# Sums of the last projection's weights computed early and kept in DRAM; eight of eleven pairs by seven products

## The chip, the cores and the metric

The kernel runs on one core of one Trainium2 chip. The metric is the device time of one execution in microseconds (us), as the median of several executions; lower is better.

## The reference, cut to what matters

One decoder layer over 512 tokens of width 1024. Three token mixers (gMLP "a", sparse attention "b", the recurrent block "c") are gated and merged, then comes a SwiGLU feed-forward part. What the change touches is the last matrix product of all, and in time the third branch.

```python
y = w_o( sum_k sigmoid(gate_k(h)) * (branch_k @ W_br_k) );  x = x + rms_norm(y)
...
f = (jax.nn.silu(f_gate) * f_up) @ w_ffn_out      # 512 x 2816  times  2816 x 1024
x = x + rms_norm(f)
...
def compress(t, pe, w1, w2):                      # of keys and of values, in branch b
    return jax.nn.gelu(flat @ w1) @ w2
```

## The kernel before, in words

**Split products.** Every large product is done in three passes on TensorE: each operand is written as a high part (rounded to fp32r) and a low part (the rest), and hi·hi, hi·lo and lo·hi are summed in PSUM. `split` (L112 to L122) makes the parts: ScalarE (ACT) copies the high part (L117), VectorE (DVE) subtracts it for the low one (L122). Weights come in 512 KB tiles of 128x1024, loaded on SyncE's queue (SP, L182) into `raw` (two buffers), then split into `hi` and `lo` (three buffers each). A main matmul is 128x128 by 128x512.

**The order of the work** is fixed when the program is built. Each engine, and each queue of DMA issues, runs its own list strictly in that order, and waits on semaphores for the others. Generators are interleaved by `run(main, side)` (L1612): `main` is a list of generators that issue matmuls, and at every yield `side` is stepped.

**The third branch.** `run(ahead, seq(compress(1), gmlp_prep(), v_norm()))` runs the eight `branch_part("c", j)` and the gate parts between them (14 parts in `ahead`), one 512 KB weight tile each; `run([u_tile(j) ...])` follows with eight more. Beside them `compress(1)` (L650) makes compressed keys or values of branch b: matmuls into a bank `tr` (L670), a GELU of which DVE does two steps into `chid` (L678, L680) and ACT the steps between (L677, L679), copies into `h4` (L694, eight) and small matmuls on `h4` (L698). The one before it, `compress(0)`, ends in the matmuls of L685, which read its `chid`. `merged` (L1035) is DVE's step that reads each branch tile out of PSUM. The hidden layer's weights `w` come by two loads of 1 MB on ACT's queue (L652).

**The last projection.** The 2816 rows of `w_ffn_out` are 11 pairs of 256 rows; tile `w_fo[i]` holds pair i for output columns 0 to 511, `w_fo[11+i]` for the others. The first NP = 5 pairs are multiplied directly (`block`, L1388): `down_first` (L1390) does columns 0 to 511, `down_last` (L1570) the rest. Of these `down_last` takes the last LAST = 4 tiles together, block of tokens by block of tokens, and closes each block (`close`, from L1579: the square on ACT into `junk`, the norm on DVE, the stores) while the next is multiplied. The other NS = 6 pairs go through seven products of half size instead of eight, on sums of quarters of the activations and of the weights (class `Seven`, products at L1493). `prep_a` (L1428) loads both tiles of a pair, makes the two weight sums on DVE (L1435, L1436), stores one of them in a DRAM tile `t2` (L1437), and splits four quarters; these feed the first sweep (four products a pair). `prep_b` (L1458) loads the other two quarters and `t2` (L1463 to L1465, 256 KB each), subtracts `t2` from both (L1470, L1471) and splits three quarters for the second sweep (three products a pair). A sweep works on one pair while the one after the next is prepared. Sums of the activations are made at L1447, L1448, L1478 and L1479.

Of the kernel before, what the change touches and what calls it, by code (L numbers as in the profile page):

```python
# [50 lines left out]
def hybrid_block(ctx: ExitStack, tc: tile.TileContext, A, out):  # L51
# [41 lines left out]
    def slab(name, dt=F32, tag="slab", shape=(4, S)):  # L93
        pool, bufs = (merge if tag == "m" else big, TAGS[tag]) if tag in TAGS else phase_pool[tag]
        return pool.tile([128, *shape], dt, tag=tag, name=nm(name), bufs=bufs)
# [20 lines left out]
    def split(src, hi, lo, lo_eng=None):  # L116
        res["hi"] = SC.activation(hi, src, AF.Copy)  # L117
        e = lo_eng or V
        if e is GP:
            GP.tensor_sub(lo, src, f32(hi))  # L120
        else:
            res["lo"] = V.tensor_sub(lo, src, f32(hi))  # L122
# [36 lines left out]
            wlist += [(A["w_vp"][1, i], None) for i in range(2)]  # L159
    w_branch(1)  # L160
    wlist += [(A["w_o"][k], t) for k, t in enumerate(["h"] * 4 + ["f"] + ["m"] * 2 + [None])]
    HEAD, LAST, LASTV = 2, 4, 2
    WAIT, STEP = (5, 6, 7), (1, 1, 2)
    wlist += [(A["w_fi"][i], None if i < 2 else "h") for i in range(2 * HEAD)]
    wstop = [len(wlist)]
    NS = 6
    NP = NFF // 2 - NS
    wlist += [(A["w_fo"][i], "y" if i < 2 else None) for i in range(NP)]
    wfirst_half = len(wlist)
# [383 lines left out]
    def v_norm():  # L553
        st = const0([128, 4, 2, 6], "bnst")
        ag = const.tile([128, 4, 2], F32, name="bnag")
        sd = const.tile([128, 2, 4], F32, name="bnsd")
        for c in range(4):
            with tc.issue_after(res["lo"].ins):
                for i in range(2):
                    V.bn_stats(st[:, c, i, :], gm["v"][c // 2][:, c % 2, i * 512:(i + 1) * 512])  # L560
            V.bn_aggr(ag[:, c, :], st[:, c])
            yield

        V.tensor_mul(sd[:, 1], ag[:, :, 1], rmul[:, 2])
        rsqrt(sd[:, 0], sd[:, 1], 4, 1.0, 4 * EPS)
        V.tensor_mul(sd[:, 0], sd[:, 0], rstd)
        V.scalar_tensor_tensor(sd[:, 1], ag[:, :, 0], -1.0, sd[:, 0], op0=OP.mult, op1=OP.mult)
        for c in range(4):
            v = gm["v"][c // 2][:, c % 2, :]
            V.tensor_scalar(v, v, sd[:, 0, c:c + 1], sd[:, 1, c:c + 1], op0=OP.mult, op1=OP.add)  # L570
            yield

    ya = {}
# [834 lines left out]
    class Seven:  # L1408


        def __init__(self):
            self.keep = slab("kS", tag="h", shape=(NS, 256))
            self.t2 = tc.dram_tile([NS, 128, 512], F32, name="t2")
            self.w, self.x = {}, {}
            self.turn = 0

# [11 lines left out]
        def prep_a(self, s):  # L1428

            i = NP + s  # L1430
            r0, r1 = self.raw()
            SY.dma_start(r0, A["w_fo"][i])
            SY.dma_start(r1, A["w_fo"][NFF // 2 + i])
            yield
            V.tensor_sub(r1[:, :512], r1[:, 512:], r1[:, :512])  # L1435
            V.tensor_add(r1[:, 512:], r0[:, :512], r1[:, :512])  # L1436
            SY.dma_start(self.t2[s], r1[:, 512:])  # L1437
            yield
            w1 = self.stream()
            split(r0, *w1)  # L1440
            yield
            w2 = slab("w2", F32R, "mo", (2, 1024))
            w2 = w2[:, 0], w2[:, 1]
            split(r1, *w2)
            yield
            F, k = fpair(i), self.keep[:, s]
            V.tensor_sub(F[:, 256:512], F[:, :256], F[:, 256:512])  # L1447
            V.tensor_sub(k, F[:, 768:], F[:, 256:512])  # L1448
            yield
            u = slab("ua", F32R, "mo", (2, 1024))  # L1450
            split(F[:, :768], u[:, 0, :768], u[:, 1, :768])
            split(k, u[:, 0, 768:], u[:, 1, 768:])
            for p, x, w, o in (("P1", 0, w1, 0), ("P7", 256, w2, 0), ("P2", 512, w1, 512), ("P6", 768, w2, 512)):
                self.x[s, p] = [u[:, l, x:x + 256] for l in range(2)]
                self.w[s, p] = [t[:, o:o + 512] for t in w]
            yield

        def prep_b(self, s):  # L1458

            i = NP + s  # L1460
            r, t2 = self.raw()
            t2 = t2[:, :512]
            SY.dma_start(r[:, :512], A["w_fo"][i, :, 512:])  # L1463
            SY.dma_start(r[:, 512:], A["w_fo"][NFF // 2 + i, :, 512:])
            SY.dma_start(t2, self.t2[s])  # L1465
            yield
            w1 = [t[:, :512] for t in self.stream()]
            split(r[:, 512:], *w1)
            yield
            V.tensor_sub(r[:, 512:], r[:, 512:], t2)  # L1470
            V.tensor_sub(r[:, :512], r[:, :512], t2)  # L1471
            yield
            w2 = slab("w3", F32R, "mo", (2, 1024))
            w2 = w2[:, 0], w2[:, 1]
            split(r, *w2)
            yield
            F, k = fpair(i), self.keep[:, s]
            V.tensor_add(F[:, 256:512], k, F[:, :256])  # L1478
            V.tensor_sub(F[:, 512:768], F[:, 512:768], k)  # L1479
            yield  # L1480
            u = slab("ub", F32R, "mo", (2, 1024))
            split(F[:, 256:], u[:, 0, :768], u[:, 1, :768])
            for p, x, w, o in (("P5", 0, w2, 512), ("P3", 256, w1, 0), ("P4", 512, w2, 0)):
                self.x[s, p] = [u[:, l, x:x + 256] for l in range(2)]
                self.w[s, p] = [t[:, o:o + 512] for t in w]
            yield
# [19 lines left out]
    def sweeps(sv):  # L1506

        b = res["b0"]
        zu = slab("zu", tag="fx")
        z, u3 = [zu[:, n, :] for n in range(2)], [zu[:, n + 2, :] for n in range(2)]  # L1510
        for n in range(2):
            SC.activation(z[n], b[2 + n], AF.Copy)
        X2, X1, X3 = b[:2], [bank("mm") for _ in range(2)], [bank("tr") for _ in range(2)]
        X4 = [bank("mm") for _ in range(2)]
        steps = iter(())

        def go(n=9):
            for _ in range(n):
                next(steps, None)

        for s in range(NS):
            end = s >= NS - 2
            for p, X in (("P1", X1), ("P6", X3), ("P7", X4)) + (() if end else (("P2", X2),)):
                sv.product(s, p, X, s == 0 and p != "P2")
                go(2)
            go()
            if not end:
                steps = sv.prep_a(s + 2)
        for s in (NS - 2, NS - 1):
            sv.product(s, "P2", X2, False)  # L1530
            steps = sv.prep_b(s - NS + 2)
            if s == NS - 2:
                p1, u2 = [[row("p1") for _ in range(2)] for _ in range(2)]
                for n in range(2):
                    SC.activation(p1[n], X1[n], AF.Copy)
                for n in range(2):
                    V.tensor_add(X3[n], X3[n], p1[n])
                for n in range(2):
                    SC.activation(u2[n], X3[n], AF.Copy)
                for n in range(2):  # L1540
                    V.tensor_add(X4[n], X4[n], u2[n])
                for n in range(2):
                    SC.activation(u3[n], X4[n], AF.Copy)
            go()
        for n in range(2):
            close_first(n, X2[n], p1[n])
        X5 = [bank("mm") for _ in range(2)]
        for s in range(NS):
            for p, X in (("P5", X5), ("P3", X3), ("P4", X4)):
                sv.product(s, p, X, s == 0 and p == "P5")  # L1550
                go(2)
                if s == NS - 1 and p == "P5":
                    p5 = [row("p5") for _ in range(2)]
                    for n in range(2):
                        SC.activation(p5[n], X5[n], AF.Copy)
                    for n in range(2):
                        V.tensor_add(X5[n], X5[n], u3[n])
                if s == NS - 1 and p == "P3":
                    for n in range(2):
                        V.tensor_add(X3[n], X3[n], p5[n])  # L1560
            go()
            if s + 2 < NS:
                steps = sv.prep_b(s + 2)
            elif s + 2 == NS:
                wstop[0] = len(wlist)
        for n in range(2):
            close_first(2 + n, X4[n], z[n])
        res["b1"] = X3 + X5
# [70 lines left out]
    def seq(*gens):  # L1639
        for g in gens:  # L1640
            for _ in g:
                yield 1
# [26 lines left out]
    run([gate_part("c", 0), compress(0), gate_part("c", 1)], side)  # L1669
    yc["h"], yc["l"] = ([yc[n, k // 4][:, k % 4, :] for k in range(NK)] for n in "hl")  # L1670
    ahead = [x for j in range(8) for x in [branch_part("c", j, yc)] + ([gate_part("c", j + 2)] if j < 6 else [])]
    run(ahead, seq(compress(1), gmlp_prep(), v_norm()))
    run([u_tile(j) for j in range(8)])
    next_phase(1)
    next_banks(1)
    for tag in ("sc", "sc", "o"):
# [120 lines left out]
```

## Time and profile before

| what | before |
|---|---|
| median of 3 runs (lowest, highest) | 1118.88 us (1118.82, 1119.29) |
| the profiled execution: its time | 1118.62 us |
| the profiled execution: its span | 1116.9 us |
| TensorE (PE) busy | 1106.0 us, 99% |
| VectorE (DVE) busy | 825.0 us, 74% |
| ScalarE (ACT) busy | 612.7 us, 55% |
| DMA, mean over the span | 110 GB/s |

The profiled execution's time is its span and 1.7 us around it. In rows of the timeline the columns are: start in us, duration in us, engine, line, operation, output and inputs, shapes, how often (xN: merged), and in brackets the idle time before it and what ended it. Rows of the stretches give busy time and count for each engine, then the granted clock, the DMA share and the rate. Matmuls overlap in the pipe: one is 0.39 us long, and the next starts before it ends. "Qs" after an engine's name (SPq, ACTq) are its DMA issues.

### The profile page before, as it was taken

To read this page: it belongs to the slowest core of one execution; us is meant where nothing else is said; L and a number is where in the kernel's file an instruction comes from. 1 tells how busy PE (TensorE), PEld (TensorE's weight loads), DVE (VectorE), ACT (ScalarE), POOL (GpSimd) and SP (SyncE) were. 2 spreads that over 40 slices of the span, in tenths; PEclk is the share of its full clock that TensorE was granted. 3 is DMA by queue.
4 is the path that set the end of the run, shared out by engine and by line. 5 is a ranking of instruction groups with operands and counts; after the bars stand their busy time and mean duration, and the time that the engine had idled before them with its cause. 6 is when DMAs were issued, how large, how long until landed. Compare 5 with 4: busy or idle time off the path is not lost.

```text
span 1116.9 us, 16130 instructions
## 1 busy us (share of the span) xinstructions
PE 1106.0 (99%) x6164; PEld 958.8 (86%) x6164; DVE 825.0 (74%) x1514; ACT 612.7 (55%) x1107; POOL 22.4 (2%) x39
## 2 busy tenths in 40 slices
PE   9999999999999999999999999999999999999997
PEld 8888788888889888888788788888999999998876
DVE  5987858263574888978888844468998888877894
ACT  6757574232344696957967633345655555563651
POOL 1000202100000000000000000000000000000000
PEclk9999999999999999999999999999999999999999
DMA  8332316323223312222221253353233323356351
GB/s 320 103 94 76 113 57 236 103 76 94 94 76 105 94 49 61 63 58 77 66 57 57 65 200 94 106 177 113 76 114 114 114 79 130 114 174 211 96 198 75
DMA packets 36572, 122.36 MB, mean 110 GB/s; under 512 B 4304, under 2 KB 4592, under 8 KB 35344
## 3 DMA queue, kind: packets, MB, share of 16 engines
q1 hardware_dynamic: 34048, 111.61, 31.0%
q10 hardware_dynamic: 2160, 9.04, 2.3%
q8 instruction: 48, 0.79, 0.3%
q0 software_dynamic: 288, 0.69, 0.2%
q14 instruction: 28, 0.23, 0.1%
HBM read 112.42 MB, written 5.77 MB: 106 GB/s over the span
## 4 chain that ended last, share of the span: by engine, by line
PE 91%; DVE 4%; ACT 3%; issue 1%; DMA 1%; DVEq 0%; ACTq 0%
PE mm L221 40%; PE mm L1292 18%; PE mm L526 4%; PE mm L1388 4%; PE sc L857 3%; PE o L895 3%; PE mm L1077 3%; PE tr L882 3%; PE mm L1493 2%; PE mm L763 2%; PE mm L234 2%; PE tr L670 1%; PE tr L1388 1%; PE tr L449 1%; PE tr L1493 1%; DVE lo L122 1%
## 5 line engine op out<-in xcount | busy, mean ns | idle before, releaser
L117 ACT ACTIVATE hi<-raw 128x1024 fp32r<-128x1024 f32 (+1 forms) x132 | 136.1, 1032 | 180.8 <-PE mm L221 99.8
L122 DVE TENSOR_TENSOR lo<-raw,hi 128x1024 fp32r<-128x1024 f32 (+1 forms) x132 | 157.1, 1192 | 90.1 <-ACT hi L117 83.7
L221 PE MATMUL mm<-hh,hi 128*128 128x512 f32 x504 | 199.6, 396 | 0.0
L221 PE MATMUL mm<-hh,lo 128*128 128x512 f32 x504 | 197.2, 391 | 0.0
L221 PE MATMUL mm<-hl,hi 128*128 128x512 f32 x504 | 196.9, 391 | 0.0
L221 PEld LDWEIGHTS mm<-hh,lo 128*128 128x128 f32 x504 | 94.7, 188 | 19.8
L221 PEld LDWEIGHTS mm<-hl,hi 128*128 128x128 f32 x504 | 94.7, 188 | 18.6 <-issue 0.2
L221 PEld LDWEIGHTS mm<-hh,hi 128*128 128x128 f32 x504 | 94.7, 188 | 18.2 <-issue 0.2
L863 ACT ACTIVATE P<-P,ast 128x128 f32<-128x128 f32 (+3 forms) x128 | 70.6, 553 | 16.0 <-DVE ast L861 15.4
L1292 PE MATMUL mm<-S,g 128*128 128x256 f32 x600 | 76.9, 283 | 0.0
L1292 PEld LDWEIGHTS mm<-S,g 128*128 128x128 f32 x600 | 74.2, 192 | 0.1
L861 DVE CUSTOM_DVE_ANT_0 P<-sc,mask 128x128 f32<-128x128 f32 (+3 forms) x128 | 58.1, 482 | 8.3 <-PE sc L857 8.1
L122 DVE TENSOR_TENSOR pl<-tr,ph 128x512 fp32r<-128x512 f32 x80 | 53.5, 685 | 12.5 <-ACT ph L117 10.6
L117 ACT ACTIVATE ph<-tr 128x512 fp32r<-128x512 f32 x80 | 46.0, 590 | 11.9 <-PE tr L882 9.2
L857 PE MATMUL sc<-K,q 128*128 128x512 f32 (+2 forms) x192 | 49.6, 365 | 0.1
L1292 PE MATMUL mm<-A,g 128*128 128x256 f32 x360 | 46.6, 283 | 0.0
L882 PE MATMUL tr<-ident,P 128*128 128x128 f32 x320 | 45.2, 273 | 0.3 <-ACT P L873 0.3
L882 PEld LDWEIGHTS tr<-ident,P 128*128 128x128 f32 x320 | 38.0, 140 | 8.2 <-ACT P L873 0.8
L1292 PEld LDWEIGHTS mm<-A,g 128*128 128x128 f32 x360 | 44.8, 192 | 0.1
L1292 PE MATMUL mm<-S,hi 128*128 128x256 f32 x240 | 44.6, 283 | 0.0
L1292 PE MATMUL mm<-A,hi 128*128 128x256 f32 x240 | 44.2, 283 | 0.0
L857 PEld LDWEIGHTS sc<-K,q 128*128 128x128 f32 x192 | 33.3, 188 | 6.4 <-DVE ast L861 1.2
(397 smaller groups left out, 2439.1 us busy)
## 6 DMA issues: line engine op xcount, KB each, us to landing
raw<-in_w_in SPq DMA_DIRECT2D x64, 512.0 KB, 3.6
raw<-in_w_fi SPq DMA_DIRECT2D x44, 512.0 KB, 3.6
raw<-in_w_br SPq DMA_DIRECT2D x24, 512.0 KB, 3.5
raw<-in_w_fo SPq DMA_DIRECT2D x22, 512.0 KB, 3.7
w<-in_cw ACTq DMA_DIRECT2D x4, 1024.0 KB, 6.0
raw<-in_w_o SPq DMA_DIRECT2D x8, 512.0 KB, 3.6
raw<-in_w_v SPq DMA_DIRECT2D x7, 512.0 KB, 5.0
raw<-in_w_fo SPq DMA_DIRECT2D x12, 256.0 KB, 3.2
```

Of the source, the lines that this page charges most:

```text
L117: res["hi"] = SC.activation(hi, src, AF.Copy)
L122: res["lo"] = V.tensor_sub(lo, src, f32(hi))
L221: res["mm"] = PE.matmul(ps[:m, n0:n1], w[:, k * 128:k * 128 + m], x[k][:, n0:n1], start=(t == 0), stop=(t == 3 * NK - 1))
L526: res["mm"] = PE.matmul(b[c], x[k][:, c * 128:(c + 1) * 128], w[:, kk * 512:kk * 512 + 512], start=(k == 0 and t == 0), stop=(k == NK - 1 ...
L857: PE.matmul(ps[:, :w * n].rearrange("p (b n) -> p b n", b=w), lhs, K[:, i, brs[0]:brs[-1] + 1, :n], start=(i == 0), stop=(i == 1))
L861: V.tensor_tensor_reduce(out=t, in0=ps[:, b * n:b * n + n], in1=mask[0][:, S - n:], scale=-0.125, scalar=3.0e38, op0=OP.add, op1=OP.min, a ...
L863: SC.activation(t, t, AF.Exp, scale=-1.0, bias=st[:, 0, j, b:b + 1], accum_out=st[:, 1, j, b:b + 1])
L882: PE.transpose(pt[:, j * 128:(j + 1) * 128], self.part(j, br)[:, kt * 128:(kt + 1) * 128], ident)
L895: PE.matmul(po, VV[:, kt, g % 2, br].rearrange("p i d -> p (i d)"), x, start=(br == 0 and kt == 0 and t == 0), stop=(br == 1 and kt == a a ...
L1077: res["mm"] = PE.matmul(b[c, f], x[k][:, q], w[:, fs], start=(k == 0 and t == 0), stop=(k == NK - 1 and t == 2))
L1292: res["mm"] = PE.matmul(ps, w[:, ks], x[:, l, k, :], start=(first and k == t == 0), stop=(k == 3 and t == 2), skip_group_check=not first)
L1388: PE.matmul(ps, x[k][:, q], w[:, ws], start=(start and kk == t == 0), stop=(kk == 1 and t == 2), skip_group_check=True)
```

## The change

- NS goes from 6 to 8, so NP from 5 to 3, and LAST from 4 to 3.
- The weight sums are no longer made in `prep_a` and `prep_b`. A generator `sums_prep` makes them ahead, into a DRAM tile `sums`: for each of the eight pairs two loads of 512 KB into a `slab` tile `fo` (L580 of the new kernel), three DVE steps (L582 and L583 128x512, L584 128x1024), two stores of 512 KB (L586), all DMAs on SP's queue. It is stepped once after each of the 14 parts of `ahead`, and after each `u_tile`. `slab` has three buffers.
- `prep_a` loads `w_fo[i]` and 512 KB of `sums`, `prep_b` a half of `w_fo` (256 KB) and 512 KB of `sums`. Neither has sums of its own any more, and `t2` is gone.
- The quarters of P6 and P7 lie the other way round; `zu` moves from tag `fx` to `h`.

```diff
-    HEAD, LAST, LASTV = 2, 4, 2
+    HEAD, LAST, LASTV = 2, 3, 2
-    NS = 6
+    NS = 8
...
+    sums = tc.dram_tile([NS, 2, 128, 2, 512], F32, name="sums")
+
+    def sums_prep():
+        for s in range(NS):
+            r = slab("fo", shape=(2, 2, 512))
+            for n in range(2):
+                SY.dma_start(r[:, n].rearrange("p a n -> p (a n)"), A["w_fo"][n * (NFF // 2) + NFF // 2 - NS + s])
+            yield
+            V.tensor_sub(r[:, 1, 0], r[:, 1, 1], r[:, 1, 0])
+            V.tensor_add(r[:, 0, 0], r[:, 0, 0], r[:, 1, 0])
+            V.tensor_tensor(r[:, :, 1], r[:, :, 1], r[:, 0:1, 0].to_broadcast([128, 2, 512]), op=OP.subtract)
+            for i in range(2):
+                SY.dma_start(sums[s, i], r[:, :, i])
+            yield
...
-            SY.dma_start(r1, A["w_fo"][NFF // 2 + i])
-            yield
-            V.tensor_sub(r1[:, :512], r1[:, 512:], r1[:, :512])
-            V.tensor_add(r1[:, 512:], r0[:, :512], r1[:, :512])
-            SY.dma_start(self.t2[s], r1[:, 512:])
+            SY.dma_start(r1.rearrange("p (a n) -> p a n", a=2), sums[s, 0])
...
-            r, t2 = self.raw()
-            t2 = t2[:, :512]
-            SY.dma_start(r[:, :512], A["w_fo"][i, :, 512:])
-            SY.dma_start(r[:, 512:], A["w_fo"][NFF // 2 + i, :, 512:])
-            SY.dma_start(t2, self.t2[s])
+            r0, r1 = self.raw()
+            SY.dma_start(r0[:, 512:], A["w_fo"][NFF // 2 + i, :, 512:])
+            SY.dma_start(r1.rearrange("p (a n) -> p a n", a=2), sums[s, 1])
...
-            V.tensor_sub(r[:, 512:], r[:, 512:], t2)
-            V.tensor_sub(r[:, :512], r[:, :512], t2)
...
-        zu = slab("zu", tag="fx")
+        zu = slab("zu", tag="h")
...
-    run(ahead, seq(compress(1), gmlp_prep(), v_norm()))
-    run([u_tile(j) for j in range(8)])
+    prep_fo = sums_prep()
+
+    def then(gen):
+        yield from gen
+        next(prep_fo, None)
+
+    run([then(x) for x in ahead], seq(compress(1), gmlp_prep(), v_norm()))
+    run([then(u_tile(j)) for j in range(8)])
```

How the built program's order moves is shown at three places. The number after a tile's name tells apart tiles of one name (`fo_1727` is the first pair's), and the last column is the shape written. The lines of `compress` and of the branch are 16 higher in the new kernel (L678 is L694, L680 is L696, L694 is L710, L1035 is L1051).

First, DVE from the first gate tile's low part in the third branch on (`lo`: low part of a weight tile; `chid`, `h`: the compression's hidden layer; `fo`: a pair's sums). Before:

```order
L122 TENSOR_TENSOR lo_1644<-raw_1641,hi_1643 128x1024
L678 SCALAR_TENSOR_TENSOR chid_1597<-chid_1597,tr_1598 128x2x124
L680 SCALAR_TENSOR_TENSOR chid_1597<-chid_1597,tr_1598 128x2x124
L122 TENSOR_TENSOR lo_1677<-raw_1674,hi_1676 128x1024
...
L509 TENSOR_SCALAR gw_1902<-gw_1902 128x512
L678 SCALAR_TENSOR_TENSOR chid_1743<-chid_1743,tr_1744 128x2x124
L680 SCALAR_TENSOR_TENSOR chid_1743<-chid_1743,tr_1744 128x2x124
L694 COPY h_279_1852<-chid_1743 128x4x31 x4
```

The same stretch of DVE in the new kernel:

```order
L122 TENSOR_TENSOR lo_1647<-raw_1644,hi_1646 128x1024
L582 TENSOR_TENSOR fo_1727<-fo_1727 128x512
L583 TENSOR_TENSOR fo_1727<-fo_1727 128x512
L584 TENSOR_TENSOR fo_1727<-fo_1727 128x2x512
L694 SCALAR_TENSOR_TENSOR chid_1600<-chid_1600,tr_1601 128x2x124
L696 SCALAR_TENSOR_TENSOR chid_1600<-chid_1600,tr_1601 128x2x124
...
L582 TENSOR_TENSOR fo_2131<-fo_2131 128x512
L694 SCALAR_TENSOR_TENSOR chid_1749<-chid_1749,tr_1750 128x2x124
L583 TENSOR_TENSOR fo_2131<-fo_2131 128x512
L696 SCALAR_TENSOR_TENSOR chid_1749<-chid_1749,tr_1750 128x2x124
L584 TENSOR_TENSOR fo_2131<-fo_2131 128x2x512
L710 COPY h_281_1866<-chid_1749 128x4x31 x4
```

The first pair's three steps stand ahead of the first `chid`, and the fifth pair's (`fo_2131`) stand among the second `chid` and ahead of the copies into `h`. Between the two places, in the part left out, stand the sums of pairs two to four.

Second, SP's queue in the same stretch, in the new kernel (before, this queue holds only the `raw` loads here, in the same order):

```order
L580 DMA fo_1727<-in_w_fo 128x1024 x2
L182 DMA raw_1731<-in_w_in 128x1024
L580 DMA fo_1826<-in_w_fo 128x1024
L586 DMA sums<-fo_1727 256x1x512 x2
L580 DMA fo_1826<-in_w_fo 128x1024
L580 DMA fo_1945<-in_w_fo 128x1024 x2
L182 DMA raw_1779<-in_w_br 128x1024
L586 DMA sums<-fo_1826 256x1x512 x2
...
L580 DMA fo_2131<-in_w_fo 128x1024
L586 DMA sums<-fo_2057 256x1x512 x2
L580 DMA fo_2131<-in_w_fo 128x1024
```

Loads of later pairs stand behind stores of earlier ones, and a store waits for DVE's sums. The third pair's loads (`fo_1945`) also wait until both stores of the first have landed.

Third, DVE at the end of the feed-forward part, where the first pairs of the last projection are prepared (`fx`, `fy`, `f`: activations; L1320 to L1326 are L1336 to L1342 in the new kernel). Before:

```order
L122 TENSOR_TENSOR u_9218<-raw_9216,u_9218 128x1024
L1435 TENSOR_TENSOR raw_1348_9429<-raw_1348_9429 128x512
L1324 TENSOR_TENSOR fx_9064<-fx_9064,mm_9075 128x256
L1436 TENSOR_TENSOR raw_1348_9429<-raw_1348_9429 128x512
L1326 TENSOR_TENSOR f_9066<-fx_9064,fy_9065 128x256
L1447 TENSOR_TENSOR f_9066<-f_9066 128x256
L1320 TENSOR_TENSOR fy_9177<-fy_9177,mm_9187 128x256
```

The same place of DVE in the new kernel:

```order
L122 TENSOR_TENSOR u_9283<-raw_9281,u_9283 128x1024
L1340 TENSOR_TENSOR fx_9129<-fx_9129,mm_9140 128x256
L122 TENSOR_TENSOR lo_9476<-raw_1348_9460,hi_9475 128x1024
L1342 TENSOR_TENSOR f_9131<-fx_9129,fy_9130 128x256
L122 TENSOR_TENSOR w_1346_9426<-raw_9407,w_1346_9426 128x1024
L1336 TENSOR_TENSOR fy_9242<-fy_9242,mm_9252 128x256
```

Between L1340 (before: L1324) and L1336 (before: L1320) stood three short steps, the second weight sum among them; now two low parts of 128x1024 stand there, the second of them (`w_1346`) on data that comes from `sums`.

More of the change, by code (lines that the diff above doesn't have):

```diff
@@ L1412, in __init__ @@
             self.keep = slab("kS", tag="h", shape=(NS, 256))
-            self.t2 = tc.dram_tile([NS, 128, 512], F32, name="t2")
             self.w, self.x = {}, {}
@@ L1452, in prep_a @@
             split(k, u[:, 0, 768:], u[:, 1, 768:])
-            for p, x, w, o in (("P1", 0, w1, 0), ("P7", 256, w2, 0), ("P2", 512, w1, 512), ("P6", 768, w2, 512)):
+            for p, x, w, o in (("P1", 0, w1, 0), ("P7", 256, w2, 512), ("P2", 512, w1, 512), ("P6", 768, w2, 0)):
                 self.x[s, p] = [u[:, l, x:x + 256] for l in range(2)]
@@ L1460, in prep_b @@
             i = NP + s
-            r, t2 = self.raw()
-            t2 = t2[:, :512]
-            SY.dma_start(r[:, :512], A["w_fo"][i, :, 512:])
-            SY.dma_start(r[:, 512:], A["w_fo"][NFF // 2 + i, :, 512:])
-            SY.dma_start(t2, self.t2[s])
+            r0, r1 = self.raw()
+            SY.dma_start(r0[:, 512:], A["w_fo"][NFF // 2 + i, :, 512:])
+            SY.dma_start(r1.rearrange("p (a n) -> p a n", a=2), sums[s, 1])
             yield
             w1 = [t[:, :512] for t in self.stream()]
[L1468 to L1471, printed above, removed]
+            split(r0[:, 512:], *w1)
             yield
@@ L1474, in prep_b @@
             w2 = w2[:, 0], w2[:, 1]
-            split(r, *w2)
+            split(r1, *w2)
             yield
```

## The prediction

> **What bounds the kernel now.** I read the head of the page first, and the share of the chain that ended last.
>
> ```profile
> span 1116.9 us, 16130 instructions
> PE 1106.0 (99%) x6164; PEld 958.8 (86%) x6164; DVE 825.0 (74%) x1514; ACT 612.7 (55%) x1107; POOL 22.4 (2%) x39
> PE 91%; DVE 4%; ACT 3%; issue 1%; DMA 1%; DVEq 0%; ACTq 0%
> ```
>
> TensorE is busy 99% of the span, and the chain is 91% its work. So two things count: how many matmuls there are, and where PE is made to wait. The other engines cost nothing until PE waits for them. The stretches that the change touches, in order: the third branch, the `u` tiles after it, the second sweep.
>
> ```profile
> core 0: us, PE busy (x) PEld busy (x) DVE busy (x) ACT busy (x) POOL busy (x), PEclk, DMA share, GB/s
> 195.00:282.00 87.00, 87.00 (x422) 72.45 (x421) 35.78 (x66) 22.20 (x31) 4.37 (x8) 1.00 0.31 95
> 282.00:365.00 83.00, 83.00 (x453) 72.14 (x452) 50.61 (x73) 34.62 (x50) 0.00 (x0) 1.00 0.30 93
> 1056.00:1085.00 29.00, 27.87 (x121) 21.98 (x120) 27.63 (x39) 19.85 (x31) 0.00 (x0) 1.00 0.53 184
> ```
>
> In the first two PE has no gap, and DVE is busy 41% and 61% of the time; in the second sweep DVE is busy 27.63 of 29 us and PE has gaps. The sums are moved from a place where DVE is short to one where it has room. A mean over a stretch doesn't say who is late in it, though.
>
> **Part 1: fewer matmuls.** How many products there are, and the price of one:
>
> ```profile
> 365.00:1117.00 752.00, 55.13 (x240) 44.87 (x240) 1.00 0.33 105
> 1023.00:1117.00 94.00, 58.22 (x252) 47.00 (x252) 0.99 0.38 129
> 1104.66 2.88 PE L1388 MATMUL mm<-u,fs 128*128 128x512 f32 x12
> 1107.38 0.39 PE L1388 MATMUL mm<-hi,fs 128*128 128x512 f32 x1
> ```
>
> The first row is L1388 alone: 240 matmuls for 5 pairs, 48 each. The second is L1493 alone: 252 for 6 pairs, 42 each. Then 3 x 48 + 8 x 42 = 480 against 492: 12 fewer. Twelve of them take 1107.38 - 1104.66 = 2.72 us from start to start. **Term: -2.72 us**, certain, since PE is the bound here.
>
> **Part 2: the stalls of the second sweep.** The matmuls of L1493 in 1056 to 1085:
>
> ```profile
> L1493 PE MATMUL mm<-w,ub x72: 388/389/504, 1056.4 to 1082.7; 128*128 128x512 f32 x72
> L1493 PE MATMUL tr<-hi,ub x24: 389/389/398, 1057.7 to 1081.3; 128*128 128x512 f32 x24
> L1493 PE MATMUL tr<-lo,ub x12: 389/389/389, 1057.9 to 1081.1; 128*128 128x512 f32 x12
>   ACT ub L117: 2.8, 3
> ```
>
> These are 72 + 24 + 12 = 108, so 107 steps of 2.72 / 12 = 0.2267 us, 24.26 us, from 1056.4 to 1082.7, which is 26.3: 2.04 us are lost. The last row says on what most: ACT's high parts of `ub`, three waits; ACT stands in turn behind DVE's steps on `raw`. What DVE does for one pair there:
>
> ```profile
> 1069.62 0.68 DVE L1470 TENSOR_TENSOR raw<-raw 128x512 f32<-128x512 f32 x1
> 1070.23 0.68 DVE L1471 TENSOR_TENSOR raw<-raw 128x512 f32<-128x512 f32 x1
> 1070.83 0.68 DVE L122 TENSOR_TENSOR lo<-raw,hi 128x512 fp32r<-128x512 f32 x1
> ...
> 1072.12 1.23 DVE L122 TENSOR_TENSOR w<-raw,w 128x1024 fp32r<-128x1024 f32 x1
> 1073.26 0.95 DVE L122 TENSOR_TENSOR ub<-f,ub 128x768 fp32r<-128x768 f32 x1
> ```
>
> That is 4.22 us, against 18 x 0.2267 = 4.08 for PE. The change takes the first two away: 2.86 us, so DVE runs ahead. Bytes loaded per pair stay (three of 256 KB before, 256 and 512 KB now). ACT's splits stay. **Term: -2.0 us**, between 0 (ACT or the loads are late in its place) and -2.04.
>
> The shorter last blocks (18 matmuls, not 24, between two closes, 1.36 us less) have cover: ACT waited for PE 12.9 us in three closes, 4.3 each.
>
> ```profile
>   ACT junk L1579: 12.9, 3
> ```
>
> **Part 3: the end of the feed-forward part.** Here two splits now stand ahead of a step that frees a PSUM bank (L1320 of the old kernel), third place in the order. DVE's rows of before, then PE's:
>
> ```profile
> 992.39 0.41 DVE L1324 TENSOR_TENSOR fx<-fx,mm 128x256 f32<-128x256 f32 x1
> ...
> 994.18 0.42 DVE L1320 TENSOR_TENSOR fy<-fy,mm 128x256 f32<-128x256 f32 x1
> ...
> 1000.71 1.22 DVE L122 TENSOR_TENSOR w<-raw,w 128x1024 fp32r<-128x1024 f32 x1
> ```
>
> ```profile
> 993.57 1.55 PE L1388 MATMUL mm<-u,fs 128*128 128x512 f32 x6
> 994.95 1.59 PE L1292 MATMUL mm<-A,g 128*128 128x256 f32 x12
> ```
>
> PE writes into that bank again at 994.95, after six matmuls of the last projection. From 992.80 DVE now does 1.22 + 0.42 + 1.22 before L1320, so that ends at about 992.80 + 2.86 + 0.42 = 996.1, or 995.8 with the overlap of short steps: PE is late by 0.9 to 1.1 us. If the first `sums` load lands late, more (2), if DVE gets ahead, less (0.3). **Term: +0.8 us.** The rest of the preparation follows 60 matmuls of the direct part (13.6 us) and has cover. The sums of the activations are the same per pair.
>
> **Part 4: what the sums cost in the third branch.** Added: 8 x 3 DVE steps, 8 x (0.68 + 0.68 + 1.23) = 20.7 us, 16 loads and 16 stores of 512 KB. DVE's free time in the two stretches (51 and 32 us) and the DMA engines' (69 and 70%) hold that. But DVE's list is in order. In the new order the first pair's three steps stand ahead of `chid` of the first compression, and the fifth pair's among those of the second, with the copies into `h` behind. PE needs both:
>
> ```profile
> 190.79 0.41 DVE L678 SCALAR_TENSOR_TENSOR chid<-chid,tr 128x248 f32<-128x248 f32 x1
> 191.68 0.41 DVE L680 SCALAR_TENSOR_TENSOR chid<-chid,tr 128x248 f32<-128x248 f32 x1 [0.48 <-ACT chid L679]
> ...
> 221.46 0.41 DVE L678 SCALAR_TENSOR_TENSOR chid<-chid,tr 128x248 f32<-128x248 f32 x1 [0.67 <-ACT chid L677]
> ...
> 222.86 1.16 DVE L694 COPY h<-chid 128x124 f32<-128x124 f32 x8
> ```
>
> PE's two readers, in the same timeline:
>
> ```profile
> 195.53 0.64 PE L685 MATMUL tr<-chid,cw 128*64 128x124 f32 x4
> ...
> 223.74 0.41 PE L698 MATMUL tr<-cw,h 128*128 128x64 f32 x2
> ```
>
> The DMA issues there, and what transfers took (the `6.2` is the one `w_in` load of 186 to 198 us, issued at 190.79; the `4.3` are the loads of 1023 to 1085, close behind one another):
>
> ```profile
> 187.94 0.33 ACTq L652 DMA_DIRECT2D w<-in_cw  x1
> 189.82 0.34 ACTq L652 DMA_DIRECT2D w<-in_cw  x1
> 190.79 0.33 SPq L182 DMA_DIRECT2D raw<-in_w_in  x1
> raw<-in_w_in SPq DMA_DIRECT2D x64, 512.0 KB, 3.6
> raw<-in_w_in SPq DMA_DIRECT2D x1, 512.0 KB, 6.2
> x<-xr SPq DMA_DIRECT2D x4, 512.0 KB, 2.6
> xr<-x SPq DMA_DIRECT2D x4, 512.0 KB, 4.1
> raw<-in_w_fo SPq DMA_DIRECT2D x5, 512.0 KB, 4.3
> ```
>
> So the first matmul on `h` (L698, in the new order five matmuls later, hence at 223.74 + 5 x 0.23 = 224.9) waits for a chain through the memory, since SP's list puts loads behind stores, and stores behind DVE. The low price of a transfer is that of one alone (load 3.6, store 2.6), the high one that of one behind others (6.2 is the `w_in` load issued at 190.79 behind the two 1 MB loads of ACT's queue). First pair's second load issued at 188.0 (after `yc` is done and its tile free): lands 191.6 / 194.2. Three steps, 2.6: 194.2 / 196.8. Store lands 2.6 / 4.1 later: 196.8 / 200.9. Third pair's loads, which wait for it, 0.4 for the second issue and 4.3: 201.5 / 205.6. Sums, `merged` and one low part, 4.5: 206.0 / 210.1. Then on SP a weight load, a store and the fourth pair's two loads, 1.2, landing 4.3 / 6.2: 211.5 / 217.5. Sums 2.6, then a store and the second load of the fifth pair, 0.8, landing 3.6 / 4.3: 218.5 / 225.2. Then the steps of DVE to the first four copies: 0.68, 0.41, 0.68, 0.41, 1.23 and 0.58: 229.2 in the high case; in the low one the matmuls before set L678 at 221.46, and the end is 221.46 + 3.3 = 224.8. **PE is late by 0 / 4.3 us.** The first `chid` (0 / 2.6 late: 196.8 + 1.3 against 195.53) makes it no longer: the chain doesn't hang on PE, so PE's first wait is a part of this one. Transfers are crowded here (from 188 to 192 some 4 MB are asked for: the two 1 MB loads, two pairs' halves, a weight), so I take a value near the high end. **Term: +4.2 us**, between 0 and 6.5 (each of the five transfers in the chain 0.45 us above its high price).
>
> [...]
>
> Sums of later pairs also stand ahead of `lo` of later weight tiles. Those are split two tiles ahead of their use, and a tile is 24 matmuls or 5.4 us and more of PE's time, so a delay of the 8 us that the chain above gives (`lo` at 202.38 before, 210.1 at worst) is covered. `merged` is as late, and its bank comes up again only later. In the `u` stage only the last pairs remain, beside DVE's 32 us of free time.
>
> **Sum.** -2.72 - 2.0 + 0.8 + 4.2 = +0.3 us on the profiled execution: its span of 1116.9 and 1.7 us around it are 1118.6, which lies 0.3 under the median of the runs shown, 1118.88. I forecast 1118.6 + 0.3 = **1118.9 us**: no change. A difference under 0.2% (2.2 us) can't be told from none here.
>
> **Rivals.**
>
> A. *The round trips are hidden.* If transfers go nearly at the price of one alone, the second `chid` and `h` come when they did. For it: mean DMA share 0.31. Against: the 6.2 row. Then -2.72 - 2.0 + 0.8 + 0 to 1.5 = -3.9 to -2.4: 1114.7 to 1116.2. Chance 0.32, faster.
>
> B. *The chain through memory is longer than its high price.* Place: SP's queue between 188 and 225 us, where a store that waits for DVE holds weight loads and the next pair behind it. Each of the five transfers 0.45 us over the high price makes 6.5, and with the end of the feed-forward part at 1.1: -2.72 - 2.0 + 1.1 + 6.5 = +2.9: 1121.5. It decides from 5.9 us of lost time in the third branch up (5.9 + 1.1 - 4.72 = 2.3). Chance 0.15, slower.
>
> C. *The second sweep's stalls stay*, because ACT and the mix of loads, not DVE's two steps, set them (the longest wait is put down to ACT's `ub`). -2.72 + 0.8 + 4.2 = +2.3: 1120.9, at the border. Chance 0.18, half of it slower, the rest no change.
>
> My forecast: 0.35. So faster 0.32 (A), slower 0.24 (B and half of C), within 0.2% 0.44. The range goes from A's low end to B, a little over on B's side: 1114.6 to 1121.6.
>
> **What would show it.** In the new profile: 144 matmuls at the direct product's line and 336 at L1499. In the second sweep no wait of PE over 0.3 us; waits there kill part 2. A wait of PE at L1404 or L1308 near 995 for DVE's `fy`: part 3. The wait at the matmuls on `h` (L714, near 225), with DVE's L582 of the fifth pair just before and that waiting for its load: part 4; if PE has no gap between 190 and 240, rival A is right. A forecast of no change would be wrong for a good reason only if one of the two large terms is off by 2 us or more; right for a bad one if both are.

## The result, and the profile after

| what | before | changed |
|---|---|---|
| median of 6 runs each (lowest, highest) | 1119.55 us (1118.82, 1121.07) | 1129.25 us (1127.96, 1130.33) |
| the profiled execution: time, span | 1118.62, 1116.9 us | 1129.31, 1127.3 us |

The change makes the kernel slower: ratio 1.0085, 95% interval 1.0072 to 1.0098. The time lies above the range given. The head of the new page:

```profile
span 1127.3 us, 16193 instructions
PE 1107.9 (98%) x6152; PEld 960.6 (85%) x6152; DVE 837.2 (74%) x1530; ACT 617.5 (55%) x1115; POOL 22.0 (2%) x39
...
PEclk9999999889999999999999999999999999999999
```

Two things stand out. There are 12 fewer matmuls (6152 against 6164), and yet PE is busy for 1.9 us more: some must have run more slowly. And in the eighth and ninth slice (197 to 254 us) the granted clock is below full speed, which no slice of before is. The waits of PE say where that begins:

```profile
PE tr L714 <- DVE h L710: 4.5, 1, 4.5
PE tr L701 <- DVE chid L696: 3.4, 1, 3.4
```

These are the two readers that part 4 named, `chid` and `h` of the third branch. PE's timeline around both (two stretches and the next landmark):

```profile
195.41 0.39 PE L221 MATMUL mm<-ycl,hi 128*128 128x512 f32 x1
199.24 1.09 PE L701 MATMUL tr<-chid,cw 128*64 128x124 f32 x4 [3.44 <-DVE chid L696]
...
200.85 0.63 PE L221 MATMUL mm<-ych,hi 128*128 128x512 f32 x1
201.28 0.63 PE L221 MATMUL mm<-ycl,hi 128*128 128x512 f32 x1
...
205.47 0.39 PE L221 MATMUL mm<-ych,lo 128*128 128x512 f32 x1
...
230.99 0.39 PE L221 MATMUL mm<-hl,hi 128*128 128x512 f32 x1
235.92 0.51 PE L714 MATMUL tr<-cw,h 128*128 128x64 f32 x2 [4.54 <-DVE h L710]
...
242.31 0.63 PE L221 MATMUL mm<-ych,hi 128*128 128x512 f32 x1
...
243.05 0.40 PE L221 MATMUL mm<-ych,lo 128*128 128x512 f32 x1
...
248.07 1.02 PE L513 MATMUL mm<-gw,ones 128*128 128x512 f32 x2
```

Behind each wait stand matmuls of 0.63 us, whose starts lie 0.43 apart (200.85 to 201.28), where others last 0.39 and start every 0.23 us. After 6 to 7 us they are back at the old pace. The stretches show the cause in the clock (seventh to ninth entry: PEclk, DMA share, GB/s):

```profile
199.00:205.00 6.00, 5.76 (x15) 4.48 (x16) 1.41 (x2) 1.71 (x4) 0.00 (x0) 0.50 0.75 280
205.00:231.00 26.00, 26.00 (x147) 22.51 (x146) 12.95 (x15) 4.05 (x5) 3.13 (x6) 0.99 0.94 327
231.00:236.00 5.00, 0.46 (x3) 0.11 (x2) 3.95 (x13) 1.36 (x2) 0.00 (x0) 1.00 0.94 382
236.00:243.00 7.00, 7.00 (x25) 6.23 (x26) 2.96 (x6) 2.73 (x6) 0.00 (x0) 0.51 0.92 307
```

The granted clock is 0.50 and 0.51 in the 6 and 7 us behind the waits. L513, a landmark right behind the second, starts 14.3 us later than in the timeline of before:

```profile
233.80 1.02 PE L513 MATMUL mm<-gw,ones 128*128 128x512 f32 x2
```

The 14.3 us are worked out from the starts. First wait: 199.24 against the 195.64 that the pace of 0.23 would give, 3.6. The matmuls after it: eleven steps of 0.43 for 0.23 and a slow start, 2.6. Second wait: 235.92 against 231.22, 4.7. The slow matmuls after that: 3.2. Together 14.1; the other 0.2 us are there before the first wait, since the new kernel reaches this stretch that much later.

From there on the distance hardly changes (15.1 us at 783 us and at 994 us of before), and then it shrinks: the last matmul starts 10.4 us later. So the last projection gained 4.65 us. Its matmuls at the direct product's line and at L1499, and the stretch of the second sweep:

```profile
1000.00:1127.00 127.00, 33.18 (x144) 26.90 (x144) 0.99 0.48 162
1000.00:1127.00 127.00, 76.32 (x336) 63.06 (x336) 0.99 0.48 162
1056.00:1092.00 36.00, 36.00 (x161) 29.80 (x160) 29.32 (x41) 23.38 (x36) 0.00 (x0) 1.00 0.55 188
```

There are 144 and 336 products, and in the sweep PE has no gap (36.00 of 36).

What held `chid` and `h` back is in DVE's timeline:

```profile
195.18 0.69 DVE L582 TENSOR_TENSOR fo<-fo 128x512 f32<-128x512 f32 x1 [4.21 <-DMA fo<-in_w_fo]
...
209.10 0.69 DVE L582 TENSOR_TENSOR fo<-fo 128x512 f32<-128x512 f32 x1 [1.15 <-DMA fo<-in_w_fo]
...
221.94 0.69 DVE L582 TENSOR_TENSOR fo<-fo 128x512 f32<-128x512 f32 x1 [4.55 <-DMA fo<-in_w_fo]
...
232.05 0.69 DVE L582 TENSOR_TENSOR fo<-fo 128x512 f32<-128x512 f32 x1 [1.89 <-DMA fo<-in_w_fo]
...
235.04 1.15 DVE L710 COPY h<-chid 128x124 f32<-128x124 f32 x8
```

These are the sums of the first, third, fourth and fifth pair. Each time DVE is idle, waits for a load of `fo`, and holds what stands behind: `chid` of the first compression behind the first row, the copies into `h` behind the fifth pair. The high prices of part 4 gave 194.2, 205.6, 217.5 and 225.2; the chain is later by 1.0, 3.5, 4.4 and 6.9 us. The transfers issued from 186 to 235 us, in the changed kernel:

```profile
fo<-in_w_fo SPq DMA_DIRECT2D x12, 512.0 KB, 6.8
sums<-fo SPq DMA_DIRECT2D x9, 512.0 KB, 5.5
w<-in_cw ACTq DMA_DIRECT2D x2, 1024.0 KB, 9.2
raw<-in_w_in SPq DMA_DIRECT2D x3, 512.0 KB, 7.3
gw<-in_bs POOLq DMA_DIRECT2D x1, 256.0 KB, 5.9
```

And the same window of before:

```profile
w<-in_cw ACTq DMA_DIRECT2D x2, 1024.0 KB, 6.0
raw<-in_w_in SPq DMA_DIRECT2D x4, 512.0 KB, 3.6
gw<-in_bs POOLq DMA_DIRECT2D x1, 256.0 KB, 3.0
```

The kinds that both have here take 1.5 to 2 times as long as before. (The load `gw<-in_wsT` of 256 KB, not shown, takes 3.4 us against 2.9.) From 205 to 236 us the new kernel keeps the DMA engines busy 94% of the time (the stretches above); in the same window of before it is 28%.

### The profile page after: what moved, and what is told of

Same layout as the page of the kernel before. It is cut to its first block, busy times and chain, and to the rows that moved or that the text cites. A ratio compares the mean times of both kernels' runs of the same rounds, so it can differ in the third digit from the quotient of the medians.

```text
span 1127.3 us, 16193 instructions
## 1 busy us (share of the span) xinstructions
PE 1107.9 (98%) x6152; PEld 960.6 (85%) x6152; DVE 837.2 (74%) x1530; ACT 617.5 (55%) x1115; POOL 22.0 (2%) x39
## 4 chain that ended last, share of the span: by engine, by line
PE 85%; DVE 6%; ACT 4%; DMA 3%; issue 1%; SPq 0%; DVEq 0%; ACTq 0%
PE mm L221 36%; PE mm L1308 18%; PE mm L1499 5%; PE mm L526 3%; PE mm L1093 3%; PE sc L873 3%; PE o L911 2%; PE tr L898 2%; PE mm L1404 2%; PE mm L779 2%; PE tr L1499 2%; PE mm L234 2%; DMA fo<-in_w_fo 2%; DVE lo L122 1%; PE tr L449 1%
## 5 line engine op out<-in xcount | busy, mean ns | idle before, releaser
L1308 PE MATMUL mm<-S,g 128*128 128x256 f32 x600 | 76.9, 283 | 0.0
L1308 PEld LDWEIGHTS mm<-S,g 128*128 128x128 f32 x600 | 74.2, 192 | 0.0
L122 DVE TENSOR_TENSOR pl<-tr,ph 128x512 fp32r<-128x512 f32 x80 | 53.5, 685 | 12.9 <-ACT ph L117 10.9
L1308 PE MATMUL mm<-A,g 128*128 128x256 f32 x360 | 46.7, 283 | 0.0
L1308 PEld LDWEIGHTS mm<-A,g 128*128 128x128 f32 x360 | 44.7, 192 | 0.3 <-DVE fy L1336 0.3
L1308 PE MATMUL mm<-S,hi 128*128 128x256 f32 x240 | 44.6, 283 | 0.0
L1308 PE MATMUL mm<-A,hi 128*128 128x256 f32 x240 | 44.2, 283 | 0.0
```

What stands on the lines that cost most here:

```text
L1308: res["mm"] = PE.matmul(ps, w[:, ks], x[:, l, k, :], start=(first and k == t == 0), stop=(k == 3 and t == 2), skip_group_check=not first)
```

## The experiments

Two theories. *Head of the list*: DVE's and GpSimd's lists are in order, and steps that wait for a transfer stand ahead of `chid` and `h`; PE then waits, and waits like the two above (3.4 and 4.5 us) also leave its clock at half (0.50 and 0.51 in the 6 and 7 us behind them). *Crowding*: the 16 MB themselves slow what the kernel needs, wherever the new steps stand. In the kernels that keep the old last projection, nothing reads `sums`.

### The sums alone

The kernel before, with the new preparation added.

```diff
+    sums = tc.dram_tile([8, 2, 128, 2, 512], F32, name="sums")
+    def sums_prep():
...
+    run([then(x) for x in ahead], seq(compress(1), gmlp_prep(), v_norm()))
+    run([then(u_tile(j)) for j in range(8)])
```

> The last projection as before (six pairs, five direct); only the eight pairs' loads, sums and stores are added in the third branch, in the changed kernel's order, and nobody reads them. Theory: the whole loss sits there, two waits of PE behind DVE's list (3.6 and 4.7 us) and about 6 us of half-speed matmuls after each, so 14.1 us slower than before, 1.0126 of its time. Rival (the new last projection is slow too, and the gain of 4.6 us read at the end of the trace is chance): about 10 us slower, as the whole change.

Measured: 1132.77 us against 1119.30 (ratio 1.0119, 1.0104 to 1.0134). PE's waits:

```profile
PE tr L701 <- DVE chid L696: 3.7, 1, 3.7
PE tr L714 <- DVE h L710: 3.2, 1, 3.2
```

The loss (13.5 us) is all there without the new last projection, at the same two places. The projection itself is a gain, of 3.8 us by the medians (13.5 against 9.7).

### The traffic alone

The same loads and stores, without DVE's three steps.

```diff
-            V.tensor_sub(r[:, 1, 0], r[:, 1, 1], r[:, 1, 0])
-            V.tensor_add(r[:, 0, 0], r[:, 0, 0], r[:, 1, 0])
-            V.tensor_tensor(r[:, :, 1], r[:, :, 1], r[:, 0:1, 0].to_broadcast([128, 2, 512]), op=OP.subtract)
```

> As the run with the sums alone, without DVE's three steps a pair: the same 16 loads and 16 stores of 512 KB in the same stretch, stores of the unchanged data. Theory (DVE's list behind late loads is what stops PE): no wait of PE at the two readers over 0.3 us, no slow matmuls, time within 1 us of before. Rival (the traffic itself slows the matmuls or delays the weight tiles): slow matmuls of 0.427 us step or waits for weights between 190 and 265 us, 4 to 6 us lost.

Measured: 1124.95 us (1.0045, 1.0028 to 1.0062), a loss that I had not expected without the steps. PE waits once, 3.0 us, for `h` (L707 here). DVE's timeline ahead of it, and below that its step on `gw` in the kernel before:

```profile
224.59 0.95 DVE L509 TENSOR_SCALAR gw<-gw 128x512 f32<-128x512 f32 x1 [3.54 <-DMA gw<-in_bs]
...
226.84 1.16 DVE L707 COPY h<-chid 128x124 f32<-128x124 f32 x8
```

```profile
220.34 0.44 DVE L509 TENSOR_SCALAR gw<-gw 128x512 f32<-128x512 f32 x1 [0.34 <-DMA gw<-in_bs]
```

A step on `gw`, a table for a later stage, stands ahead of `chid`. As long as its load took 3.0 us, DVE waited 0.34 us for it and `h` came in time; here the load takes 6.3 us, and DVE waits 3.54. GpSimd's list has the same form: a step on `gw` whose load takes 5.5 us here, and 2.9 in the kernel before, stands ahead of the memset for `h`. So far this fits both theories.

### The traffic, with the steps on `gw` behind

`issue_after` puts an instruction behind the named ones in the order.

```diff
-        GP.affine_select(wsT, wsT, pattern=[[0, G], [1, 128]], compare_op=OP.is_ge, fill=0.0,
-                         base=0, channel_multiplier=-1)
-        V.tensor_scalar(rwb[:, 1], rwb[:, 1], 0.5, None, op0=OP.mult)
+        with tc.issue_after(res["ms"].ins), tc.issue_after(res["h4"].ins):
+            GP.affine_select(wsT, wsT, pattern=[[0, G], [1, 128]], compare_op=OP.is_ge, fill=0.0,
+                             base=0, channel_multiplier=-1)
+            V.tensor_scalar(rwb[:, 1], rwb[:, 1], 0.5, None, op0=OP.mult)
...
```

> The traffic alone again, with DVE's step on gw put behind the copies into h, and GpSimd's step on gw behind its memsets of h; all else as in the run with the traffic alone. Theory (traffic cost 3.2 us and slow matmuls only through the late gw loads, for which DVE and GpSimd wait in order ahead of h): no wait at the matmuls on h over 0.5 us, no slow matmuls, time within 1 us of before. Rival (traffic delays PE in another way too): 2 us or more slower.

Measured: 1119.78 us against 1119.25 (1.0005, 0.9996 to 1.0014). All the traffic is there, and the stretches show PE without a gap at full clock while the DMA engines are full (a share of 1.01):

```profile
206.00:222.00 16.00, 16.00 (x100) 14.16 (x99) 3.45 (x4) 2.98 (x4) 2.56 (x5) 1.00 1.01 376
```

That decides for the head of the list: in this run the crowding costs PE nothing by itself. It makes transfers late (the load `gw<-in_wsT` takes 5.6 us here, 2.9 before), and that costs where a list that PE needs waits for one of them.

### One pair alone

The run with the sums alone, with the first of its eight pairs only.

```diff
-        for s in range(8):
+        for s in range(1):
```

> Only the first pair's loads, sums and stores are added to the kernel before, so only the first wait can come. Theory (a gap of over about 3 us makes TensorE run at half clock for about 6 us): wait 3.5 us, then matmuls at 0.427 us for about 6 us, 2.6 to 3.0 us more: 6.1 to 6.5 us slower than before. Rival (only the wait costs; the slow matmuls came with the heavy traffic, which is gone here): 3.5 us slower, all matmuls at 0.227.

Measured: 1125.39 us (1.0055, 1.004 to 1.007), +6.1 us for a single pair of eight. PE's timeline:

```profile
198.99 0.64 PE L701 MATMUL tr<-chid,cw 128*64 128x124 f32 x4 [3.29 <-DVE chid L696]
...
200.44 0.63 PE L221 MATMUL mm<-ych,lo 128*128 128x512 f32 x1
...
203.77 0.39 PE L221 MATMUL mm<-ycl,hi 128*128 128x512 f32 x1
```

The wait (3.4 us) makes a good half of the loss; slow matmuls from 200.1 to 203.5 us, about half as long as I had expected, add 1.9 in this execution (1124.69 us, the fastest of four).

### Half a pair, and shorter steps

To make the same wait shorter: two loads of 256 KB for 512, DVE's steps as before; then the third step of 128x512; then that and one more step of 256 or 512 columns. (The sums are of other halves.)

```diff
-                SY.dma_start(r[:, n].rearrange("p a n -> p (a n)"), A["w_fo"][n * (NFF // 2) + NFF // 2 - 8 + s])
+                SY.dma_start(r[:, n, 0], A["w_fo"][n * (NFF // 2) + NFF // 2 - 8 + s][:, :512])
...
-            V.tensor_tensor(r[:, :, 1], r[:, :, 1], r[:, 0:1, 0].to_broadcast([128, 2, 512]), op=OP.subtract)
+            V.tensor_sub(r[:, 1, 0], r[:, 0, 0], r[:, 1, 0])
+            V.tensor_sub(r[:, 1, 0, :256], r[:, 0, 0, :256], r[:, 1, 0, :256])
```

The half pair:

> As the run with one pair, with two loads of 256 KB instead of 512 KB, the same three steps of DVE on them and the same stores, so a shorter wait. Theory: data about 1.3 us sooner, wait about 2.2 us, too short for the clock to fall, so 2.2 us slower and all matmuls at 0.227. Rival (any wait of some us brings the half clock): 2.2 + 2.6 = 4.8 us slower, with a stretch at 0.427.

The third step shorter, with the theory of the half pair (no slow matmuls) against a rival again:

> The half pair's run with the third DVE step of 128x512 in place of 128x1024, 0.54 us less, so a wait of about 2.5 us after 3.06 there. [...] Rival (2 us are enough): 2.5 + 2.5 = 5 us slower with a stretch at 0.427.

One more step of 256 columns, and one of 512:

> The run with the middle-sized half pair and one DVE step of 128x256 more ahead of chid, 0.42 us, so a wait of about 1.9 us (1.5 in that run). If the clock falls only for gaps near 3 us: all matmuls at 0.227. If 2 us are enough: a stretch at 0.427.

> As the run before it, with the added DVE step of 128x512, 0.68 us, so a wait of about 2.2 us, between the 1.5 that left the clock alone and the 3.06 that brought it down. Near 3 us is the point: all matmuls at 0.227; else a stretch at 0.427.

Measured: 1124.22 us (1.0043, 1.0027 to 1.0059) for the half pair, 1121.88 us (1.0025, 1.0016 to 1.0035) with the short third step, and one execution each of the last two: 1120.90 and 1124.42 us. PE's wait at `chid` in the four kernels, in this order (L702 is L701):

```profile
198.62 1.09 PE L701 MATMUL tr<-chid,cw 128*64 128x124 f32 x4 [2.90 <-DVE chid L696]
```

```profile
197.93 0.64 PE L701 MATMUL tr<-chid,cw 128*64 128x124 f32 x4 [1.38 <-DVE chid L696]
```

```profile
PE tr L702 <- DVE chid L697: 1.4, 1, 1.4
```

```profile
PE tr L702 <- DVE chid L697: 3.2, 1, 3.2
```

None of the four waits is the one that the kernel was built for (2.2, 2.5, 1.9 and 2.2 us). Half the bytes did not halve the wait: with 256 KB it is still 2.9, and the loss of 4.9 us is what the rival gave, not the theory. After the waits of 1.4 every matmul keeps its 0.23 us; after those of 2.9 and 3.2 there is a stretch at half clock (in 198 to 206 us the granted clock is 0.57 in the half pair and 0.79 in the last kernel, and 1.00 in the two others). The half pair's own executions show it too: their mean clock and time were 0.995, 0.996, 0.998, 0.999 and 1126.26, 1124.27, 1124.17, 1122.17 us, so the same kernel differs by 4.1 us with the clock; the last, 2.9 us above the kernel before, would fit the wait alone. The load lands at another time in each, and PE is ready at another: L582 starts at 194.56, 194.39, 193.20 and 194.37 us in the four, and PE's wait begins at 195.7, 196.6, 195.8 and 195.5. Between 1.4 and 2.9 us nothing was measured. Of the 2.6 us that the short third step loses, the wait explains 1.4; the rest stays open.

### The sums behind the critical readers

The changed kernel, with the sums begun after the fourth part of `ahead`, their loads and stores behind the latest weight load in SP's list, and their steps behind the latest `lo` in DVE's.

```diff
-                (SC if i == n == 0 else SY).dma_start(raw[:, p], ap[:, p])
+                res["raw"] = (SC if i == n == 0 else SY).dma_start(raw[:, p], ap[:, p])
...
+            with tc.issue_after(res["raw"].ins):
+                for n in range(2):
...
+            with tc.issue_after(res["lo"].ins), tc.issue_after(res["raw"].ins):
+                V.tensor_sub(r[:, 1, 0], r[:, 1, 1], r[:, 1, 0])
...
-    run([then(x) for x in ahead], seq(compress(1), gmlp_prep(), v_norm()))
+    run(ahead[:4] + [then(x) for x in ahead[4:]], seq(compress(1), gmlp_prep(), v_norm()))
```

> The changed kernel, with the sums started only after the fourth part of the third branch, and each pair's loads, stores and DVE steps put in the queues behind the latest weight tile's, so that neither they nor their traffic comes before the second chid and the copies into h. Theory (the loss is the two waits, the traffic ahead of them and the half clock after them; the last projection gains 4.65 us): no wait of PE over 0.5 us from 186 to 365, no slow matmuls, 4 to 4.7 us faster than before, 0.996 of its time. Rival (the sums cost PE wherever they stand, since DVE or the weight loads come late beside 8 MB loaded and 8 MB stored): waits elsewhere in the third branch or the u stage, over 2 us, no gain.

Measured: 1115.46 us (1115.11 to 1115.50) against 1119.25 (0.9966, 0.9953 to 0.9979): 3.8 us faster than the kernel before, and so 13.5 faster than the changed one (3.8 and 9.7). Its stretches:

```profile
186.00:235.00 49.00, 49.00 (x274) 41.70 (x272) 18.31 (x29) 15.06 (x25) 5.77 (x9) 1.00 0.45 155
235.00:282.00 47.00, 47.00 (x208) 38.85 (x207) 35.15 (x61) 11.03 (x13) 0.00 (x0) 1.00 0.80 282
282.00:365.00 83.00, 83.00 (x452) 72.11 (x451) 56.45 (x83) 34.25 (x50) 1.18 (x2) 1.00 0.50 169
```

PE has no gap in 179 us, and the clock is full. The bytes are the same; most now move after 235 us, where DVE has time and PE waits for nothing that stands behind them. This run moves both the order and the traffic; the next one keeps the traffic early.

### Early traffic, late steps

To tell the traffic's time from DVE's order: loads start where the change put them, but DVE's sums of the first three pairs stand behind the first `chid`, those of the others behind the copies into `h`, and the steps on `gw` behind too.

```diff
+            with tc.issue_after((res["chid"] if s < 3 else res["h4"]).ins):
+                V.tensor_sub(r[:, 1, 0], r[:, 1, 1], r[:, 1, 0])
...
+        g = V.scalar_tensor_tensor(h, t, 1.0, pv, op0=OP.add, op1=OP.mult)
+        if kv == 0:
+            res["chid"] = g
...
```

> The changed kernel with its early loads and stores, and three places in the queues changed: DVE's sums of the first three pairs stand behind the first chid, those of the others behind the copies into h, and the steps on gw (DVE and GpSimd) behind the copies and memsets of h. Theory (only what stands ahead of chid and h in an in-order queue costs, neither DVE's time nor the traffic): no wait over 0.5 us at the two readers, no slow matmuls, and the gain of the run with the late sums, 3.8 us faster than before, within 1 us of that run. Rival (early traffic or DVE's time costs by itself): 2 us or more slower than the run with the late sums.

Measured: 1117.81 us (1116.52 to 1120.40) against 1119.18 (0.999, 0.998 to 0.9999). The timelines show the one wait that is left, DVE's and then PE's:

```profile
218.15 0.69 DVE L584 TENSOR_TENSOR fo<-fo 128x512 f32<-128x512 f32 x1 [7.24 <-DMA fo<-in_w_fo]
...
222.84 0.40 DVE L696 SCALAR_TENSOR_TENSOR chid<-chid,tr 128x248 f32<-128x248 f32 x1
```

```profile
225.12 0.41 PE L718 MATMUL tr<-cw,h 128*128 128x64 f32 x2 [1.36 <-DVE h L714]
```

The DMA engines are as full as in the changed kernel (92% from 205 to 236 us, against 94%), and the order in the lists of DVE and GpSimd wins back 11.1 of the 13.5 us (9.7 and 1.4). The run is still 2.4 us slower than the one with the late sums, more than the 1 us of the theory and past the rival's mark of 2. What is left is again a place in the order: the third pair stands ahead of the second `chid`, and PE waits 1.4 us for `h` in the profiled execution (1116.52, where the run with the late sums has 1115.11). In the executions at 1120.3 and 1120.4 us the mean clock was 0.995, against 0.998 in the profiled one, which would fit a longer wait with a half-clock stretch behind it; their traces were not taken, so that is not shown.

### Eight pairs, sums in place

The kernel before with eight pairs in seven products, the sums made in `prep_a` and `prep_b` as before.

```diff
-    HEAD, LAST, LASTV = 2, 4, 2
+    HEAD, LAST, LASTV = 2, 3, 2
-    NS = 6
+    NS = 8
...
-        zu = slab("zu", tag="fx")
+        zu = slab("zu", tag="h")
```

> Eight pairs by seven products, with the weight sums made where they were (prep_a, prep_b); nothing in the third branch. Theory (the stalls of the second sweep come from the two DVE steps a pair, so they grow with the pairs): 2.72 us of matmuls saved, stalls 2.0 x 8 / 6 = 2.7 in place of 2.0, so 2.0 us faster than before; if DVE's 6.0 us a pair of the first sweep against PE's 5.44 piles up over eight pairs, up to 2 us slower. Rival (the stalls are an accident of the first pairs): 2.7 us faster, stalls as before.

Measured: 1117.55 us (0.9986, 0.9977 to 0.9995), -1.7 us. PE's waits:

```profile
PE mm L1493 <- ACT ub L117: 1.1, 1, 1.1
PE mm L1292 <- DVE fy L1320: 0.6, 1, 0.6
```

The stall of the second sweep is 1.1 as with six pairs, and from the starts, worked out as in part 2, 2.2 in all: it does not grow with the pairs to 2.7, as the theory had it. PE's one gap comes ahead of the sweep's third pair, here as before. The second row is at the place of part 3: a sum in place and a low part stand ahead of `fy`. 2.72 - 0.6 is 2.1, near the 1.7 measured.

## Why the prediction was wrong

**Part 1** held: 144 and 336 products, twelve fewer. Part 1 and part 2 together were put at 4.7 us, and the last projection gained 4.65. It gains the same in the traces of the two kernels with the sums moved: 4.65 with the late sums and 4.64 with the early traffic, from the starts of the same matmuls.

**Part 2** held in its number: no gap of PE in the second sweep. That the sums from memory do it, not the number of pairs, follows from the eight pairs with sums in place, which still have 2.2 us of stalls. Rival C is out. The reason given was too simple: if DVE's 4.22 us a pair against PE's 4.08 set the stalls, they would grow with the pairs, and they don't. Also, the row with three waits for `ub` counts PE's weight loads; PE itself waits once, for 1.1 us. Which of the removed steps and loads ends the stall was not tested.

**Part 3** was too dear: 0.8 forecast, 0.07 us found. DVE was as late as forecast: its L1336 starts at 1010.97 us, 995.9 on the clock of before (15.06 less), against 995.4 to 995.7 in the working. But PE came later too:

```profile
1008.63 2.91 PE L1404 MATMUL mm<-u,fs 128*128 128x512 f32 x12
1011.45 1.70 PE L1308 MATMUL mm<-A,g 128*128 128x256 f32 x12
```

Before, six matmuls of the last projection stood ahead of that L1308; now twelve do, 1.4 us more. The order of PE's list at this place was read for DVE alone.

**Part 4** is the step that failed. Its place and kind were right: the chain through stores, loads and DVE's list, with `h` behind the fifth pair, and PE's first wait as a part of the second one. But it was put at +4.2 us (at most 6.5), and the third branch lost 14.1. Two steps of the working failed.

First, the price of a transfer under this load. The four loads of the chain took 7.2, 4.6, 6.9 and 6.8 us from issue to landing where the high case has 6.2, 4.3, 6.2 and 4.3, and its store 6.1 where it has 4.1: 6.5 us more. I took as the high price what the trace of before had shown behind two other loads, but the change itself fills the DMA engines, with 21 more transfers of 512 KB in 49 us. At its end the chain was 6.7 us later than in the high case (235.92 against 229.2), and with the 4.3 of that case `h` came 11 us late. The 0.2 us of the later start are in that; the rest is 3.6 + 2.6 + 4.7 = 10.9, wait, slow matmuls, wait. This is rival B: its decision point of 5.9 us was passed, and its price of 6.5 was far too low.

Second, PE's clock, which the sum left out. The 2.6 us behind the first wait are hidden in the 10.9, since the chain didn't hang on PE. The 3.2 behind the second are on top: 10.9 + 3.2 = 14.1. The rows to see it by: 0.43 us from start to start, clock 0.50. In the changed kernel the granted clock is 0.50 for 6.83 us at each of the two waits (198.53 to 205.36 and 236.08 to 242.91 us). In the 8 us from 198 to 206 it averages 0.79 with one pair and 0.57 with the half pair; at half clock while it is low, that makes about 3.4 and 6.9 us. The wait ahead of it was 3.3 us with one pair, and 2.9 was enough in the half pair's profiled execution. The forecast had a wait of 4.3 us in it and no price for what came behind. The trace of before has no row with such a price: PE's longest wait there is 1.1 us.

The sum as measured: -4.65 + 14.1 + 0.2 (the later start) + some 0.8 us in stages the change doesn't touch = 10.45, near the 10.4 by which the spans of the two profiled executions differ (1127.3 and 1116.9). Most of the 0.8 come in two steps of 0.3 and 0.4 us, near 480 and 780 us of before; the run with the traffic and `gw` behind has steps of 0.2 at both. What they are stays open; the kernel before differs by 2.2 us between its own runs.

That the bytes cost PE time only through the order is shown by four runs: all the traffic without a loss (1119.78), a single pair that loses 6.1 us where its wait is long (1125.39), the whole change with its traffic early and its steps moved back (1117.81), and with both moved back (1115.46). What the clock does behind a wait between 1.4 and 2.9 us was not measured.

## What to carry to other kernels

Before work with a transfer ahead of it goes into a free stretch, go through each in-order list for what will stand behind its first waiting instruction, steps that have nothing to do with the change included (here `gw`): in the changed kernel DVE was busy 74% of the span, and its free time was worth nothing to `chid` and `h`, which stood behind waits for loads. Price an added transfer by what the window will be like with the change in it, not as it was. And in the traces of these runs every wait of TensorE of 2.9 to 4.5 us had a stretch at half clock with it, which cost 1.9 us (one pair), 2.6 and 3.2 (the changed kernel) on top of the wait itself, so put such work behind the last step that TensorE needs soon: that turned 9.7 us of loss into 3.8 of gain.

## What the hardware showed beyond that

- Median landing times from 186 to 235 us, with the DMA engines 35% busy before and 88% busy in the changed kernel: 512 KB loads of `w_in` 3.6 and 7.3 us, 1 MB loads 6.0 and 9.2, a 256 KB load on GpSimd's queue 3.0 and 5.9.
- Halving the first pair's loads from 512 to 256 KB took only 0.4 us off the wait behind them (3.3 to 2.9), beside two 1 MB loads in flight.
- After a wait the clock doesn't always fall at once: with one pair, PE restarted at 198.99 us and its first main matmuls started 0.33 and 0.23 apart, and from 200.44 on 0.43; in the changed kernel the clock was at 0.50 from 198.53, ahead of the restart at 199.24, and at the second wait from 236.08, behind the restart at 235.92. The low clock lasted 6.83 us twice in the changed kernel; the averages of the stretches give about 6.8 twice for the sums alone, about 6.9 for the half pair, and about 3.4 for one pair, for the traffic alone and for the half pair with 512 columns more.
